# Choosing a head's sixteen experts on a grid of 112 sums and reading the two key numbers separately

## The chip, the cores and the metric

The kernel runs on one core of a Trainium2 chip. The metric is the device time of one execution in microseconds. Of the kernel before there are three timed runs, with a median of 3425.85 us (3422.84 to 3432.39). The engines are named as the profile names them: PE multiplies matrices (PEld is its weight load), DVE is the vector engine, ACT the scalar engine, POOL the GpSimd engine, and SP issues DMAs.

## What is computed

One block of a network over 1024 tokens and 16 prepended ones: an mLSTM and a forgetting attention side by side, an output projection, and then a retrieval of experts. The last part is the one that is changed. For each token and each of 8 heads, two halves of a query are scored against 128 keys each. The 16 best of each half are kept, all pairs of them are summed, and the 16 best sums name 16 experts out of 16384:

```python
val, idx = lax.top_k(scores, PEER_TOPK)
cand = (val[:, :, 0, :, None] + val[:, :, 1, None, :]).reshape(tb, PEER_HEADS, PEER_TOPK * PEER_TOPK)
cand_id = (idx[:, :, 0, :, None] * N_KEYS + idx[:, :, 1, None, :]).reshape(tb, PEER_HEADS, PEER_TOPK * PEER_TOPK)
top_s, pos = lax.top_k(cand, PEER_TOPK)
ids = jnp.take_along_axis(cand_id, pos, axis=-1).reshape(tb, PEER_HEADS * PEER_TOPK)
gate = jax.nn.softmax(top_s, axis=-1).reshape(tb, PEER_HEADS * PEER_TOPK)
...
act = jax.nn.gelu(jnp.einsum('ted,td->te', u, xb).astype(jnp.float32), approximate=False)
w = (gate * act).astype(xb.dtype)
return jnp.einsum('te,ted->td', w, v_emb[ids])
```

Since both lists of 16 are sorted from the best down, the pair (a, c) can be among the 16 best sums only if (a + 1)(c + 1) is at most 16. Fifty pairs fulfil that.

## The kernel before

The 1024 tokens are worked on in four segments of 256 (two blocks of 128 tokens, one token to a partition). A segment passes through its projections (proj), the mLSTM and the attention (mlstm, fox), the output projection and normalization (outp), and the choice of experts (topk). Then its experts are applied in one of two ways. Segments 0 and 3 fetch the rows of their experts from memory with indirect DMAs on POOL: a row of u for every choice (ask, L329, tile gu), which DVE multiplies with the token and sums (L338; for one block POOL multiplies 5 of 16, L335), and later four rows of v per group of tokens (L365, tile gv), which PE weighs and sums (L387, tile po). Segments 1 and 2 compute all 16384 experts densely in the last part of the program (dense_u, dense_v), with their choices spread out beforehand into a table G by the function gates: DVE, ACT and POOL make one-hot factors A and B (L1153, L1156, L1161), PE multiplies them (L1163, gout), ACT copies the result (L1165), and a DMA stores it (L1167, tile gd). One of the four B of each step is POOL's, the other three are DVE's. Besides, part of the dense first half is computed ahead into memory (spill, L999 to L1002, products at L293).

The function topk goes over the 8 heads: projections of the query (L886), scores (L891), and on DVE the 16 best of each half by two rounds of MAX, MAX_INDEX and MATCH_REPLACE over 128 scores (L898 to L903). Then it calls select once for each segment, so select runs 4 x 8 = 32 times, each time for two blocks. In select the 50 sums are laid out in rows of falling length by seven additions (L919 to L928, tile cand), and their expert numbers by seven more (tile cid, after L914 has multiplied the first half's numbers by 128). The 16 best of the 50 are taken by the same two rounds (L933 to L938), which give positions from 0 to 49 (pos). To read out the numbers at these positions, for each block and each 8 of the 16 positions a one-hot of 8 x 50 is made (L947), multiplied by cid (L949) and summed (L950); L951 turns the sums into integers in the table idx. Segment 0's choice runs beside segment 1's mLSTM and attention, that of segments 1 and 2 (one topk of both) beside segment 3's mLSTM and attention, and that of segment 3 beside the gates of segments 1 and 2 (L1194 to L1195).

What order the instructions have on each engine is not the order of the code: the program is recorded, and a planner with a simulated timeline then decides how the instructions of independent parts stand on each engine. On the chip each engine takes its instructions in that order. Segment 0's fetching of rows is recorded last (gather_first, L1196) and put by the planner into gaps; it may not start ahead of the end of segment 1's normalization (L1019). So a change of one function's instructions can move others.

Of the kernel before, what the change touches and what calls it, by code (L numbers as in the profile page):

```python
# [9 lines left out]
F32 = mybir.dt.float32  # L10
F32R = mybir.dt.float32r
I32 = mybir.dt.int32
U32 = mybir.dt.uint32
AF = mybir.ActivationFunctionType
OP = mybir.AluOpType
AX = mybir.AxisListType
# [3 lines left out]
P = 128  # L20
# [9 lines left out]
NH_P = 8  # L30
TOPK = 16
NE = 16384
NCAND = [(a, TOPK // (a + 1)) for a in range(TOPK)]
CAND = sum(n for _, n in NCAND)


def block_kernel(tc, I, out, dbg=None):
    nc = tc.nc
    with ExitStack() as ctx:
        _block_kernel(ctx, tc, nc, I, out, dbg)  # L40
# [44 lines left out]

RATE = 1.08
LAG = 5

OHB = 8
RAW = 4  # L90
WH = 2

# [1 line left out]
def _block_kernel(ctx, tc, nc, I, out, dbg):  # L94

    def pool(name, bufs, stack=ctx, **kw):
        return stack.enter_context(tc.tile_pool(name=name, bufs=bufs, **kw))
# [16 lines left out]
    tk = pool("topk", 2, mid)  # L114
# [24 lines left out]
    dve, act, pe, pool_e, sync = nc.vector, nc.scalar, nc.tensor, nc.gpsimd, nc.sync  # L139
# [33 lines left out]
    pool_e.iota(iota_i, pattern=[[1, P]], base=0, channel_multiplier=0)  # L173
    iota = cp.tile([P, P], F32, tag="iota", name="iota")
    dve.tensor_copy(iota, iota_i)
    iota_c = iota[:, 0:CAND]

    def tables(name):

# [84 lines left out]
    for i in range(3):  # L264
        c = slice(i * 512, min(L, i * 512 + 512))
# [644 lines left out]
    def select(h, S, val, ixu):  # L910
            nb, idx_i, gate = NB, S.idx, S.gate
            ixf = tk.tile([P, nb, 2, TOPK], F32, tag="ixf", name="ixf")
            dve.tensor_copy(ixf, ixu)
            dve.tensor_scalar(ixf[:, :, 0, :], ixf[:, :, 0, :], 128.0, None, op0=OP.mult)  # L914
            cand = tk.tile([P, nb, CAND], F32, tag="cand", name="cand")
            cid = tk.tile([P, nb, CAND], F32, tag="cid", name="cid", bufs=1)
            for dst, src in ((cand, val), (cid, ixf)):
                o = 0
                for a, nc_ in NCAND[:5]:  # L919
                    dve.tensor_tensor(dst[:, :, o:o + nc_], src[:, :, 0, a:a + 1].broadcast_to([P, nb, nc_]),  # L920
                                      src[:, :, 1, 0:nc_], op=OP.add)
                    o += nc_
                dve.tensor_tensor(dst[:, :, o:o + 6].rearrange("p b (a c) -> p b a c", a=3),
                                  src[:, :, 0, 5:8].unsqueeze(3).broadcast_to([P, nb, 3, 2]),
                                  src[:, :, 1, 0:2].unsqueeze(2).broadcast_to([P, nb, 3, 2]), op=OP.add)
                o += 6
                dve.tensor_tensor(dst[:, :, o:o + 8], src[:, :, 0, 8:16],
                                  src[:, :, 1, 0:1].broadcast_to([P, nb, 8]), op=OP.add)  # L928
            hs = slice(h * TOPK, (h + 1) * TOPK)
            top = gate[:, :, hs]  # L930
            pos = tk.tile([P, nb, TOPK], U32, tag="pos", name="pos", bufs=1)
            for b in range(nb):
                dve.max(top[:, b, 0:8], cand[:, b, :])  # L933
                dve.max_index(pos[:, b, 0:8], top[:, b, 0:8], cand[:, b, :])
                c2 = tk.tile([P, CAND], F32, tag="c2", name="c2")
                dve.match_replace(c2, top[:, b, 0:8], cand[:, b, :], -3.0e38)
                dve.max(top[:, b, 8:16], c2)
                dve.max_index(pos[:, b, 8:16], top[:, b, 8:16], c2)  # L938
            posf = tk.tile([P, nb, TOPK], F32, tag="posf", name="posf", bufs=1)
            dve.tensor_copy(posf, pos)  # L940
            idf = tk.tile([P, nb, TOPK], F32, tag="idfh", name="idfh", bufs=1)

            bc = [P, OHB, CAND]
            for b in range(nb):
                for r in range(0, TOPK, OHB):
                    oh = tk.tile(bc, F32, tag="oh", name="oh", bufs=1)
                    dve.tensor_tensor(oh, iota_c.unsqueeze(1).broadcast_to(bc),  # L947
                                      posf[:, b, r:r + OHB].unsqueeze(2).broadcast_to(bc), op=OP.is_equal)
                    dve.tensor_tensor(oh, oh, cid[:, b, :].unsqueeze(1).broadcast_to(bc), op=OP.mult)  # L949
                    dve.tensor_reduce(idf[:, b, r:r + OHB], oh, axis=AX.X, op=OP.add)  # L950
                dve.tensor_copy(idx_i[:, b, hs], idf[:, b, :])  # L951

    def softmax(S):
        nb, gate = NB, S.gate
# [26 lines left out]
    def main(S):  # L981
        yield from fox(S)
        yield from outp(S)
    def part(g, n):
        for _ in range(n):
            next(g)
            yield
# [76 lines left out]
    def chain(*gens):  # L1064
        for g in gens:
            yield from g
# [5 lines left out]
    for i in range(-1, len(SEGS)):  # L1072
# [3 lines left out]
        w = []  # L1076
# [5 lines left out]
        if i >= 0:  # L1082
# [10 lines left out]
            m, c = main(S), 8 + 3  # L1093
            if i == 0:
                T0 = topk(segs[0])
                m, c = chain(m, part(T0, T00)), c + T00
# [16 lines left out]
    nb, xb0, nx = 2 * NB, sum(SEGS[:DENSE[0]]), DX  # L1113
# [209 lines left out]
```

## Time and profile before

One execution was profiled. Its own time is 3424.24 us, and its span from the first to the last instruction 3422.4 us.

| | kernel before |
|---|---|
| median of 3 runs | 3425.85 us |
| profiled execution | 3424.24 us |
| its span | 3422.4 us |
| mean granted clock of PE | 0.926 |
| PE busy | 3040.1 us (89%) |
| DVE busy | 2294.6 us (67%) |
| POOL busy | 1523.4 us (45%) |
| ACT busy | 1066.8 us (31%) |
| DMA moved | 931.23 MB, mean 272 GB/s |

How to read it: the span has a front of about 2128 us, in which the four segments pass, segment 0's rows are fetched and the gates are made, and a dense part of about 1294 us, in which PE multiplies without a break worth naming. A share of busy time over the span says little, since the stages have different limits; the prediction goes stage by stage. In the views that are quoted, a row of a stage has the busy microseconds of each engine (with the number of its instructions as x), then the granted clock, the DMA engines' share, and GB/s. A row of a group has the line, engine, operation, output and inputs with their sizes, the number of instructions, their busy time and mean duration in ns, and then the idle time of the engine just ahead of them.

### The profile page before, as it was taken

How to read it: one execution, taken by the hardware profiler on the slowest of the kernel's cores; microseconds unless marked ns; L12 is line 12 of the kernel's file. 1: busy time of each engine (PE TensorE's matmuls, PEld its weight loads, DVE VectorE, ACT ScalarE, POOL GpSimd, SP SyncE). 2: the span in 40 equal slices, each digit the busy share in tenths (PEclk: the TensorE clock that was granted, in tenths of full speed). 3: DMA queues.
4: the chain of work that ended last, by engine and by line, in shares of the span. 5: the costliest groups of instructions: out<-in, count | busy, mean ns of one | idle time of the engine just before them, and what ended most of it. 6: DMA issues, size and time to landing. Idle time of an engine off the chain costs nothing. (4 is left out here: it accounts for less than half of the span.)

```text
span 3422.4 us, 42278 instructions
## 1 busy us (share of the span) xinstructions
PE 3040.1 (89%) x14225; PEld 2220.2 (65%) x14225; DVE 2294.6 (67%) x5970; ACT 1066.8 (31%) x2007; POOL 1523.4 (45%) x1321
## 2 busy tenths in 40 slices
PE   8899899878768868999998775999999999999999
PEld 4566677545535646676766553777777777777666
DVE  3242678577667999776788546788767677775443
ACT  1323424233333212222444553222322232322221
POOL 1000011177875777433565675454444545444442
PEclk9998899879679888999998886999999999999999
DMA  4444445579989999866787887888889999998995
GB/s 135 131 126 137 144 145 149 167 240 315 250 299 331 328 334 346 252 242 234 283 325 280 316 302 284 287 311 314 307 310 344 345 348 343 353 342 308 339 333 205
DMA packets 373821, 931.23 MB, mean 272 GB/s; under 512 B 57268, under 2 KB 143508, under 8 KB 371556
## 3 DMA queue, kind: packets, MB, share of 16 engines
q0 software_dynamic: 161216, 552.56, 45.9%
q1 hardware_dynamic: 212388, 375.96, 32.7%
q8 instruction: 113, 1.85, 0.2%
q14 instruction: 104, 0.85, 0.1%
HBM read 860.91 MB, written 67.47 MB: 271 GB/s over the span
## 5 line engine op out<-in xcount | busy, mean ns | idle before, releaser
L329 POOL DMA_INDIRECT gu<-in_peer_u,idx x512 | 626.3, 1223 | 521.1 <-PE vo L1258 110.0
L365 POOL DMA_INDIRECT gv<-in_peer_v,idT x512 | 546.0, 1066 | 593.1 <-PE po L387 314.3
L338 DVE SCALAR_TENSOR_TENSOR gu<-gu,xng 128x1024 f32<-128x1024 f32 x472 | 592.5, 1274 | 62.5 <-DMA gu<-in_peer_u,idx 60.6
L282 ACT CAST wh<-raw 128x1024 fp32r<-128x1024 f32 x288 | 302.1, 1049 | 884.2 <-PE vo L1258 270.9
L287 DVE TENSOR_TENSOR wl<-raw,wh 128x1024 fp32r<-128x1024 f32 x262 | 320.5, 1223 | 283.0 <-ACT wh L282 250.5
L1258 PE MATMUL vo<-wh,Wh 128*128 128x512 f32 x1024 | 376.7, 396 | 34.9 <-ACT Wh L1239 18.1
L1258 PE MATMUL vo<-wl,Wh 128*128 128x512 f32 x1024 | 402.6, 393 | 0.0
L1258 PE MATMUL vo<-wh,Wl 128*128 128x512 f32 x1024 | 400.3, 392 | 0.0
L387 PE MATMUL po<-gv,Z 128*32 128x512 f32 x2048 | 262.7, 606 | 19.1 <-DMA gv<-in_peer_v,idT 18.9
L306 PE MATMUL fp<-hnh,raw 128*128 128x256 f32 (+1 forms) x1024 | 251.4, 404 | 22.3 <-DVE frs L633 11.3
L1258 PEld LDWEIGHTS vo<-wh,Wh 128*128 128x128 f32 x1024 | 194.1, 190 | 98.3 <-issue 23.3
L293 PE MATMUL du<-xl,wh 128*128 128x512 f32 x640 | 250.3, 391 | 0.0
L293 PE MATMUL du<-xh,wl 128*128 128x512 f32 x640 | 250.2, 391 | 0.0
L293 PE MATMUL du<-xh,wh 128*128 128x512 f32 x640 | 249.8, 390 | 0.0
L306 PEld LDWEIGHTS fp<-hnh,raw 128*128 128x128 f32 x1024 | 203.8, 203 | 60.5 <-DVE frs L633 12.7
L1258 PEld LDWEIGHTS vo<-wl,Wh 128*128 128x128 f32 x1024 | 193.8, 189 | 48.6 <-issue 8.4
L1258 PEld LDWEIGHTS vo<-wh,Wl 128*128 128x128 f32 x1024 | 193.2, 189 | 48.1 <-issue 7.5
L1163 PE MATMUL gout<-A,B 128*128 128x128 f32 x1024 | 164.0, 319 | 67.6 <-POOL B L1161 62.9
L1163 PEld LDWEIGHTS gout<-A,B 128*128 128x128 f32 x1024 | 150.9, 226 | 103.6 <-POOL B L1161 76.6
L1165 ACT COPY G<-gout 128x512 f32<-128x512 f32 x128 | 136.4, 1066 | 202.0 <-PE gout L1163 195.4
L433 PE MATMUL tk<-raw,hnh 128*128 128x512 f32 (+1 forms) x416 | 197.4, 623 | 2.0 <-ACT vp L576 1.8
L1263 DVE TENSOR_TENSOR acc<-acc,vo 128x512 f32<-128x512 f32 x256 | 167.0, 683 | 32.8 <-PE vo L1258 29.1
(409 smaller groups left out, 5397.5 us busy)
## 6 DMA issues: line engine op xcount, KB each, us to landing
raw<-in_ut SPq DMA_DIRECT2D x128, 512.0 KB
raw<-in_peer_v SPq DMA_DIRECT2D x128, 512.0 KB
raw<-in_wf SPq DMA_DIRECT2D x64, 512.0 KB
gd<-G SPq DMA_DIRECT2D x16, 2048.0 KB
Gt<-gd SPq DMA_DIRECT2D x32, 1024.0 KB
raw<-in_wt SPq DMA_DIRECT2D x48, 512.0 KB
raw<-in_wq SPq DMA_DIRECT2D x48, 512.0 KB
raw<-in_wo SPq DMA_DIRECT2D x32, 512.0 KB
```

The source lines that it names most:

```text
L282: seen["act"] = act.copy(h, raw)
L287: seen["dve"] = dve.tensor_sub(l, raw, h.bitcast(F32))
L293: seen["pe"] = pe.matmul(o, w, x[:, c], start=(first and i == 0), stop=(last and i == 2))
L306: pe.matmul(o, raw[:, k * P:(k + 1) * P], xh[:, k, c], start=(k == 0), stop=(k == KT - 1))
L329: d = pool_e.indirect_dma_start(out=t, out_offset=None, in_=I["peer_u"], in_offset=bass.IndirectOffsetOnAxis(ap=S.idx[:, lb, r:r + 1], axi ...
L338: dve.scalar_tensor_tensor(t, t, 1.0, xn[0], op0=OP.mult, op1=OP.mult, accum_out=G.actv[:, r:r + 1])
L365: d = pool_e.indirect_dma_start(out=t, out_offset=None, in_=I["peer_v"], in_offset=bass.IndirectOffsetOnAxis(ap=S.idT[lb][:, tok:tok + 1], ...
L387: last = pe.matmul(G.po[32 * q_:32 * q_ + 32, n, :], z[:, q_, 31 - j:63 - j], rows[q_][:, n * 512:(n + 1) * 512], start=(j == 0), stop=(j ...
L433: pe.matmul(b[0:w, :], xh[:, k, s0:s0 + w], raw[:, k % 2 * 512:(k % 2 + 1) * 512], start=(k == 0), stop=(k == KT - 1))
L1163: pe.matmul(bk[:, u * P:(u + 1) * P], B[:, u, :], A[:, u, :], start=True, stop=True)
L1258: seen["pe"] = pe.matmul(bks[b], w[:, cw], v, start=(ii == 0 and i == 0), stop=(ii == GRP - 1 and i == 2))
L1263: dve.tensor_add(o, o, bks[b])
```

## The change

The candidates are laid out on a grid of 112 sums: all 16 partners for the best four of the first half, and the first four partners for the other twelve. The grid holds all fifty pairs. It is filled by two additions. A position p on it gives back its row and column by arithmetic: the row is the greater of p shifted right by 4 and (p shifted right by 2) - 12, and the column is p less the smaller of 16 x row and 4 x row + 48. The table cid of numbers goes away: row and column are each read out of the list of 16 numbers of their half, by a one-hot of 2 x 16 x 16 for each block, and a last instruction makes 128 x first + second as an integer. The second round of the choice works in place on cand.

```diff
-NCAND = [(a, TOPK // (a + 1)) for a in range(TOPK)]
-CAND = sum(n for _, n in NCAND)
+CAND = 4 * TOPK + 12 * 4
...
             dve.tensor_copy(ixf, ixu)
-            dve.tensor_scalar(ixf[:, :, 0, :], ixf[:, :, 0, :], 128.0, None, op0=OP.mult)
-            for dst, src in ((cand, val), (cid, ixf)):
-                o = 0
-                for a, nc_ in NCAND[:5]:
-                    dve.tensor_tensor(dst[:, :, o:o + nc_], src[:, :, 0, a:a + 1].broadcast_to([P, nb, nc_]),
-                                      src[:, :, 1, 0:nc_], op=OP.add)
...
+            for a0, a1, w in ((0, 4, TOPK), (4, TOPK, 4)):
+                bc = [P, nb, a1 - a0, w]
+                dve.tensor_tensor(cand[:, :, 48 * (a0 > 0) + a0 * 4:][:, :, 0:(a1 - a0) * w].rearrange("p b (a c) -> p b a c", c=w),
+                                  val[:, :, 0, a0:a1].unsqueeze(3).broadcast_to(bc),
+                                  val[:, :, 1, 0:w].unsqueeze(2).broadcast_to(bc), op=OP.add)
...
+            for k, n in ((1, 4), (2, 2)):
+                dve.tensor_scalar(pos[:, k], pos[:, 0], n, None, op0=OP.logical_shift_right)
+            pf = tk.tile([P, 3, nb, TOPK], F32, tag="posf", name="posf", bufs=1)
+            dve.tensor_copy(pf, pos)
+            dve.scalar_tensor_tensor(pf[:, 1], pf[:, 2], 12.0, pf[:, 1], op0=OP.subtract, op1=OP.max)
+
+            dve.tensor_scalar(pf[:, 2], pf[:, 1], 4.0, 48.0, op0=OP.mult, op1=OP.add)
+            dve.scalar_tensor_tensor(pf[:, 2], pf[:, 1], 16.0, pf[:, 2], op0=OP.mult, op1=OP.min)
+            dve.tensor_sub(pf[:, 2], pf[:, 0], pf[:, 2])
...
-            bc = [P, OHB, CAND]
             for b in range(nb):
-                for r in range(0, TOPK, OHB):
-                    oh = tk.tile(bc, F32, tag="oh", name="oh", bufs=1)
-                    dve.tensor_tensor(oh, iota_c.unsqueeze(1).broadcast_to(bc),
-                                      posf[:, b, r:r + OHB].unsqueeze(2).broadcast_to(bc), op=OP.is_equal)
-                    dve.tensor_tensor(oh, oh, cid[:, b, :].unsqueeze(1).broadcast_to(bc), op=OP.mult)
-                    dve.tensor_reduce(idf[:, b, r:r + OHB], oh, axis=AX.X, op=OP.add)
-                dve.tensor_copy(idx_i[:, b, hs], idf[:, b, :])
+                oh = tk.tile(bc, F32, tag="oh", name="oh", bufs=1)
+                dve.tensor_tensor(oh, iota[:, 0:TOPK].unsqueeze(1).unsqueeze(1).broadcast_to(bc),
+                                  pf[:, 1:3, b, :].unsqueeze(3).broadcast_to(bc), op=OP.is_equal)
+                dve.tensor_tensor(oh, oh, ixf[:, b].unsqueeze(2).broadcast_to(bc), op=OP.mult)
+                dve.tensor_reduce(idf[:, b], oh, axis=AX.X, op=OP.add)
+            dve.scalar_tensor_tensor(idx_i[:, :, hs], idf[:, :, 0, :], 128.0, idf[:, :, 1, :], op0=OP.mult, op1=OP.add)
```

The line numbers of the changed kernel are smaller: by 3 from the constants to select, and by 5 behind it.

**DVE, the first head of segment 0's choice.** These rows stand on DVE where the first select reads out its numbers, beside segment 1's mLSTM and the small projections of segment 2 (other lines). Before, from the conversion of the positions:

```order
L940 CAST posf<-pos 128x32
L692 SCALAR_TENSOR_TENSOR y<-nu__2316,sm,og 128x128 x3
L947 TENSOR_TENSOR oh<-iota,posf 128x400
L692 SCALAR_TENSOR_TENSOR y<-nu__2316,sm,og 128x128
L707 SCALAR_TENSOR_TENSOR Cst<-Cst,dec,mst 128x129
L949 TENSOR_TENSOR oh<-oh,cid 128x400
L508 SCALAR_TENSOR_TENSOR rb<-gx,ra 72x256
L950 TENSOR_REDUCE idfh<-oh 128x8
```

Now, at the same place:

```order
L929 TENSOR_SCALAR pos<-pos 128x32 x2
L497 SCALAR_TENSOR_TENSOR ra<-gx 72x256
L931 CAST posf<-pos 128x96
L704 SCALAR_TENSOR_TENSOR Cst<-Cst,dec,mst 128x129
L932 SCALAR_TENSOR_TENSOR posf<-posf 128x32
L934 TENSOR_SCALAR posf<-posf 128x32
L935 SCALAR_TENSOR_TENSOR posf<-posf 128x32
L936 TENSOR_TENSOR posf<-posf 128x32
L942 TENSOR_TENSOR oh<-iota,posf 128x512
L944 TENSOR_TENSOR oh<-oh,ixf 128x512
L505 SCALAR_TENSOR_TENSOR rb<-gx,ra 72x256
L945 TENSOR_REDUCE idfh<-oh 128x32
```

Six small instructions have come ahead of the read-out, and a round of the read-out has 512 elements where it had 400; there are two rounds in a select where there were four.

**POOL, during segment 3's attention.** kqa is the operand of an attention head, loaded by a DMA that POOL issues; gu and gv are segment 0's fetched rows, and wl is the lower half of a weight. Before, up to the load of the third head:

```order
L329 DMA gu<-in_peer_u,idx 128x1024 x13
L285 TENSOR_TENSOR wl<-raw,wh 128x1024
L329 DMA gu<-in_peer_u,idx 128x1024 x14
L285 TENSOR_TENSOR wl<-raw,wh 128x1024
L329 DMA gu<-in_peer_u,idx 128x1024 x5
L365 DMA gv<-in_peer_v,idT 128x1024 x4
L329 DMA gu<-in_peer_u,idx 128x1024 x10
L365 DMA gv<-in_peer_v,idT 128x1024 x4
L329 DMA gu<-in_peer_u,idx 128x1024
L285 TENSOR_TENSOR wl<-raw,wh 128x1024
L329 DMA gu<-in_peer_u,idx 128x1024 x3
L733 DMA kqa<-kd 66x2x1040
```

Now, up to the same load:

```order
L326 DMA gu<-in_peer_u,idx 128x1024 x14
L282 TENSOR_TENSOR wl<-raw,wh 128x1024
L326 DMA gu<-in_peer_u,idx 128x1024 x13
L282 TENSOR_TENSOR wl<-raw,wh 128x1024
L326 DMA gu<-in_peer_u,idx 128x1024 x4
L362 DMA gv<-in_peer_v,idT 128x1024 x4
L326 DMA gu<-in_peer_u,idx 128x1024 x8
L362 DMA gv<-in_peer_v,idT 128x1024 x4
L326 DMA gu<-in_peer_u,idx 128x1024 x2
L282 TENSOR_TENSOR wl<-raw,wh 128x1024
L326 DMA gu<-in_peer_u,idx 128x1024 x5
L730 DMA kqa<-kd 66x2x1040
```

Counted from the beginning of the program, 215 fetches of u stand ahead of this load before and 189 now; ahead of PE's first gout stand 224 po products (28 groups of four rows of v) before and now.

**POOL, at the end of the gates.** B is POOL's one of the four factors of a step. Before, up to the last B:

```order
L365 DMA gv<-in_peer_v,idT 128x1024 x4
L1161 TENSOR_SCALAR B<-iota,jT,gT 128x128
L329 DMA gu<-in_peer_u,idx 128x1024 x3
L1161 TENSOR_SCALAR B<-iota,jT,gT 128x128
L329 DMA gu<-in_peer_u,idx 128x1024 x3
L1161 TENSOR_SCALAR B<-iota,jT,gT 128x128 x4
L329 DMA gu<-in_peer_u,idx 128x1024 x6
L1161 TENSOR_SCALAR B<-iota,jT,gT 128x128
L329 DMA gu<-in_peer_u,idx 128x1024
```

Now, up to the last B and beyond it:

```order
L1156 TENSOR_SCALAR B<-iota,jT,gT 128x128
L326 DMA gu<-in_peer_u,idx 128x1024 x2
L1156 TENSOR_SCALAR B<-iota,jT,gT 128x128 x8
L362 DMA gv<-in_peer_v,idT 128x1024 x4
L1156 TENSOR_SCALAR B<-iota,jT,gT 128x128 x2
L326 DMA gu<-in_peer_u,idx 128x1024 x5
L1156 TENSOR_SCALAR B<-iota,jT,gT 128x128
L326 DMA gu<-in_peer_u,idx 128x1024 x121
```

The gu of these rows are segment 3's. Ahead of the last B stand 19 of them before and 7 now. On PE, 276 of the 512 gout products stand behind the last product of the spill before, and 256 now; 136 po products stand behind it in both. From the first dense product on, PE's order is the same in both. ACT loads its function tables 28 times before and 26 times now: the two loads that fall away stood between segment 2's Silu (L605) and an Exp of the attention (L781).

More of the change, by code (lines that the diff above doesn't have):

```diff
@@ L87 @@
 LAG = 5
-OHB = 8
 RAW = 4
@@ L175, in _block_kernel @@
     dve.tensor_copy(iota, iota_i)
-    iota_c = iota[:, 0:CAND]
     def tables(name):
@@ L913, in select @@
             dve.tensor_copy(ixf, ixu)
-            dve.tensor_scalar(ixf[:, :, 0, :], ixf[:, :, 0, :], 128.0, None, op0=OP.mult)
-            cand = tk.tile([P, nb, CAND], F32, tag="cand", name="cand")
-            cid = tk.tile([P, nb, CAND], F32, tag="cid", name="cid", bufs=1)
-            for dst, src in ((cand, val), (cid, ixf)):
-                o = 0
-                for a, nc_ in NCAND[:5]:
-                    dve.tensor_tensor(dst[:, :, o:o + nc_], src[:, :, 0, a:a + 1].broadcast_to([P, nb, nc_]),
-                                      src[:, :, 1, 0:nc_], op=OP.add)
[L922 to L928, printed above, removed]
+            cand = tk.tile([P, nb, CAND], F32, tag="cand", name="cand", bufs=1)
@@ L929, in select @@
+            for a0, a1, w in ((0, 4, TOPK), (4, TOPK, 4)):
[3 more added lines that the diff above has]
+                                  val[:, :, 1, 0:w].unsqueeze(2).broadcast_to(bc), op=OP.add)
             hs = slice(h * TOPK, (h + 1) * TOPK)
             top = gate[:, :, hs]
-            pos = tk.tile([P, nb, TOPK], U32, tag="pos", name="pos", bufs=1)
+            pos = tk.tile([P, 3, nb, TOPK], U32, tag="pos", name="pos", bufs=1)
@@ L932, in select @@
             for b in range(nb):
[L933 to L936, printed above, removed]
+                c2 = cand[:, b, :]
+                dve.max(top[:, b, 0:8], c2)
+                dve.max_index(pos[:, 0, b, 0:8], top[:, b, 0:8], c2)
+                dve.match_replace(c2, top[:, b, 0:8], c2, -3.0e38)
@@ L937, in select @@
                 dve.max(top[:, b, 8:16], c2)
[L938 to L941, printed above, removed]
-            bc = [P, OHB, CAND]
-            for b in range(nb):
-                for r in range(0, TOPK, OHB):
-                    oh = tk.tile(bc, F32, tag="oh", name="oh", bufs=1)
-                    dve.tensor_tensor(oh, iota_c.unsqueeze(1).broadcast_to(bc),
-                                      posf[:, b, r:r + OHB].unsqueeze(2).broadcast_to(bc), op=OP.is_equal)
-                    dve.tensor_tensor(oh, oh, cid[:, b, :].unsqueeze(1).broadcast_to(bc), op=OP.mult)
-                    dve.tensor_reduce(idf[:, b, r:r + OHB], oh, axis=AX.X, op=OP.add)
-                dve.tensor_copy(idx_i[:, b, hs], idf[:, b, :])
+                dve.max_index(pos[:, 0, b, 8:16], top[:, b, 8:16], c2)
@@ new lines, in select @@
+            dve.tensor_sub(pf[:, 2], pf[:, 0], pf[:, 2])
+            idf = tk.tile([P, nb, 2, TOPK], F32, tag="idfh", name="idfh", bufs=1)
+            bc = [P, 2, TOPK, TOPK]
+            for b in range(nb):
+                oh = tk.tile(bc, F32, tag="oh", name="oh", bufs=1)
[3 more added lines that the diff above has]
+                dve.tensor_reduce(idf[:, b], oh, axis=AX.X, op=OP.add)
```

## The prediction

> **What bounds the kernel now.** I read the page first (PE 89% busy, DVE 67%), and then cut the span into stages, because such shares mean little over work with different limits. The cuts follow where the selects and the gates lie. Columns: busy us of PE, PEld, DVE, ACT, POOL, granted clock of PE, DMA share, GB/s.
>
> ```profile
> 0.00:350.00 350.00, 321.73 (x1174) 206.37 (x1175) 119.53 (x371) 101.50 (x268) 25.02 (x57) 0.93 0.47 135
> 350.00:650.00 300.00, 267.83 (x1341) 209.12 (x1340) 222.51 (x900) 104.53 (x248) 22.93 (x21) 0.91 0.47 139
> 650.00:1075.00 425.00, 307.21 (x1130) 206.30 (x1129) 273.81 (x507) 139.61 (x328) 300.54 (x216) 0.80 0.87 278
> 1075.00:1375.00 300.00, 240.76 (x1117) 185.99 (x1116) 296.14 (x945) 70.65 (x140) 214.18 (x162) 0.86 0.97 337
> 1375.00:1650.00 275.00, 259.43 (x1277) 180.64 (x1276) 186.52 (x752) 70.20 (x124) 98.16 (x87) 0.97 0.74 248
> 1650.00:1910.00 260.00, 240.18 (x1408) 179.02 (x1407) 224.52 (x920) 115.88 (x228) 150.92 (x146) 0.95 0.79 293
> 1910.00:2128.00 218.00, 132.24 (x796) 94.52 (x795) 114.79 (x316) 105.39 (x213) 149.03 (x141) 0.78 0.82 302
> 2128.00:3422.00 1294.00, 1270.67 (x5994) 958.20 (x5994) 856.75 (x1264) 359.05 (x461) 562.65 (x493) 0.99 0.89 319
> ```
>
> The last 1294 us are PE's (1271 busy) and keep their order, so nothing is to be had there. Of the rest, PE is the limit up to 350, and nearly so from 1375 to 1910. From 1075 to 1375 DVE is busy 296 of 300 us, PE only 241. From 1910 to 2128 neither is full. The same stages with the second product of the read-out alone (L949, four to a select) tell where the selects are:
>
> ```profile
> 350.00:650.00 300.00, 18.23 (x32) 0.91 0.47 139
> ...
> 1075.00:1375.00 300.00, 18.50 (x30) 0.86 0.97 337
> 1375.00:1650.00 275.00, 22.27 (x34) 0.97 0.74 248
> 1650.00:1910.00 260.00, 18.38 (x32) 0.95 0.79 293
> ```
>
> So 8, 7.5, 8.5 and 8 of the 32 selects. In DVE's own stage, these are PE's waits:
>
> ```profile
> PE fm L747 <- DVE mx L753: 15.1, 7, 5.3
> PE sc L891 <- ACT qT L888: 9.2, 3, 6.8
> PE fmT L758 <- DVE Zm L755: 7.6, 2, 4.9
> PE mst L706 <- DVE Cst L707: 7.3, 3, 5.1
> ...
> PE fmT L758 <- DVE mx L753: 3.4, 2, 2.5
> ```
>
> Those on DVE add up to 15.1 + 7.6 + 7.3 + 3.4 = 33 us of the 59 us that PE stands idle: attention and mLSTM wait for small DVE results that are queued behind row sums and selects.
>
> **What one select costs DVE, before and after.** The groups by shape, and DVE in order of time in one select:
>
> ```profile
> L949 DVE TENSOR_TENSOR oh<-oh,cid 128x400 f32<-128x400 f32 x128 | 77.4, 605 | 1.9
> L950 DVE TENSOR_REDUCE idfh<-oh 128x8 f32<-128x400 f32 x128 | 71.8, 561 | 1.6
> L899 DVE FIND_INDEX8 ixu<-val,sc 128x8 uint32<-128x128 f32 x128 | 35.1, 283 | 0.0
> L934 DVE FIND_INDEX8 pos<-gate,cand 128x8 uint32<-128x50 f32 x64 | 13.1, 204 | 0.0
> L676 DVE TENSOR_TENSOR nu__4858<-nu__4858,m 128x129 f32<-128x129 f32 x4 | 1.2, 288 | 2.6 <-issue 1.9 <-ACT nu__4858 L675 0.7
> L914 DVE TENSOR_SCALAR ixf<-ixf 128x32 f32<-128x32 f32 x32 | 5.7, 179 | 0.0
> ```
>
> ```profile
> 510.63 0.50 DVE L920 TENSOR_TENSOR cid<-ixf 128x32 f32<-128x32 f32 x5
> 511.05 0.16 DVE L923 TENSOR_TENSOR cid<-ixf 128x12 f32<-128x12 f32 x1
> ...
> 513.68 0.57 DVE L949 TENSOR_TENSOR oh<-oh,cid 128x400 f32<-128x400 f32 x1
> 514.29 0.57 DVE L950 TENSOR_REDUCE idfh<-oh 128x8 f32<-128x400 f32 x1
> 514.89 0.57 DVE L947 TENSOR_TENSOR oh<-iota,posf 128x400 f32<-128x400 f32 x1
> ```
>
> - An element costs (283 - 204) / (128 - 50) = 1.01 ns.
> - Read-out: dependent steps start 0.605 us apart (513.68, 514.29, 514.89). Before 12 of them, 7.26 us. Now 6 with 112 elements more, 0.605 + 0.113 = 0.72 us each, 4.31 us. Saved 2.95.
> - Small additions: five start within 511.05 - 510.63 = 0.42 us, so 0.084 each, independent ones overlapping in part. Fourteen of them and L914 are 15 x 0.084 = 1.26 us. The two new ones have 2 x 4 x 16 = 128 and 2 x 12 x 4 = 96 elements; by the 128x129 row (288 ns, less about 0.07 of overlap) 0.40 us for both. Saved 0.86.
> - The choice of 16: ten passes over 62 elements more, 10 x 62 x 1.01 ns. Added 0.63. They take the same loads of match values as before.
> - Undoing the position: six more small instructions and 64 more elements in the conversion. Overlapped they would cost 6 x 0.084 = 0.5 us, as a strict chain 6 x 0.18 (L914) = 1.08. It is nearly a chain, so 0.9 + 0.06; nothing but DVE's other work can stand between.
> - The end: two conversions become one instruction of the same kind. Saved 0.1.
>
> Sum 2.95 + 0.86 - 0.63 - 0.96 + 0.1 = 2.3 us of DVE for a select, 74 us over 32. Ends: 1.7 (two-input products at 0.76, the strict chain), and 3.4 if each removed addition had held DVE for its whole duration of 0.16.
>
> The Trainium skill, "VectorE: DVE Perf Modes", section "The DRAIN you can't avoid", has the next instruction wait until the pipe is empty and advises a smaller count of instructions; the same page lets one that is not held start earlier. By the first rule alone the sum would be the upper end, 3.4 us a select. The row of five additions in 0.50 us speaks for the second.
>
> **What of it reaches the end.**
>
> Segment 0's choice (350 to 650): 8 x 2.3 = 18 us less of 222 on DVE. PE is idle 32 us there, and its waits on DVE are:
>
> ```profile
> PE fp L306 <- DVE frs L633: 8.2, 2, 5.8
> ...
> PE fmT L758 <- DVE mx L753: 3.1, 2, 2.8
> ```
>
> That is 11.3 us; I take 4, between nothing and 11, nearer to DVE's share of the load that goes. Two table loads on ACT go as well; ACT is busy 105 of the 300 us and hides them.
>
> DVE's stage (1075 to 1375): 7.5 x 2.3 = 17 us less. DVE is full, so its chain gets shorter by that; PE gets back the part of its idle time that hangs on DVE, 33 of 59. I take 0.6 x 17 = 10, between 0 (if the fetches hold) and 17.
>
> From 1375 to 1650 PE is the limit (259 of 275): the 20 us of DVE that go there were cover already. 0.
>
> Gates, first part (1650 to 1910): PE has 240 of 260. The planner puts five more steps of the gates ahead of the last spill product (256 gout products behind it in place of 276). Twenty products cost PE 20 x 2 x 0.16 = 6 us there (two records to a product, and 164.0 us for 1024 records):
>
> ```profile
> L1163 PE MATMUL gout<-A,B 128*128 128x128 f32 x1024 | 164.0, 319 | 67.6 <-POOL B L1161 62.9
> ```
>
> Loss 6, gain by lighter DVE up to 6; I take -4.
>
> Gates, second part (1910 to 2112): POOL's groups in this stretch, busy and then idle time ahead of them, fill it:
>
> ```profile
> L1161 POOL TENSOR_SCALAR B<-iota,jT,gT 128x128 f32<-128x128 f32 x65 | 69.2, 1067 | 21.0 <-PE gout L1163 19.2 <-DMA gv<-in_peer_v,idT 0.5 <-POOL B L1161 0.2
> L365 POOL DMA_INDIRECT gv<-in_peer_v,idT x57 | 57.4, 1008 | 26.5 <-PE po L387 14.2 <-issue 9.7 <-PE gout L1163 2.3
> L329 POOL DMA_INDIRECT gu<-in_peer_u,idx x19 | 23.0, 1213 | 4.7 <-issue 3.4 <-DVE B L1161 0.5 <-DVE A L1153 0.5
> ```
>
> 69.2 + 21.0 + 57.4 + 26.5 + 23.0 + 4.7 = 202 us: POOL's queue is the stage. A B takes 90.2 / 65 = 1.39 us with its wait, a gu 27.7 / 19 = 1.46. The changed order has 5 B and 12 gu fewer ahead of its last B: 5 x 1.39 + 12 x 1.46 = 24.5. The gu go behind the last B, where POOL now stands idle. I take 20, between 0 and 24.
>
> Sum: 4 + 10 + 0 - 4 + 20 = 30 us. The profiled execution took 3424.24 us (span 3422.4 and 1.8 around it), 1.6 below the median of 3425.85. Forecast 3424 - 30 = **3394 us**; with the ends of the terms set against each other, 3375 to 3408.
>
> **Rivals.**
>
> *The fetches hold.* From 1075 to 1375 the DMA share is 0.97 at 337 GB/s; a lighter DVE would only wait for rows. Against it: from 1910 to 2128 a share of 0.82 moved 302 GB/s, so a full share may move 368, 9% more. Then that term is 0, POOL's order gives half of its 20, and the first part of the gates still loses 4: 4 + 0 - 4 + 10 = 10 us, 3414 us. Chance 0.20.
>
> *The clock comes along.* PE's granted clock is 0.86 in DVE's stage, where PE idles, and 0.99 in the tail, where it doesn't. With the waits on DVE gone, 241 us of products at 0.86 would take 241 x 0.86 / 0.95 = 218 (0.95 as from 1650 to 1910). With 17 us in place of 10 and half of those 23 us: 30 + 7 + 12 = 49, 3375 us. Chance 0.12. The Trainium skill, "TensorE: Matmul & The Clock Gate", section "Part 1: The HAM clock gate (the "warmup" mystery)", says that the clock halves after an idle window of about 3.4 us and comes back with activity; the waits of 4.9 to 5.3 us above are of the length that it means.
>
> *PE comes too early (slower).* Between 1075 and 1910 PE's products for segment 0 (po) stand at fixed places in its order, 28 groups ahead of the first gout, and the third attention head of segment 3 now stands behind 189 fetches of u, not 215. PE moves up against fetches that can't, and then holds everything behind a po. It decides from 30 / 28 = 1.1 us of added wait per group; at 1.6 us it costs 45, and the time is 3394 + 45 = 3439 us. Against it: DMA has a share of only 0.74 from 1375 to 1650. Chance 0.10.
>
> *DVE isn't lighter.* If the chain for the positions and the longer choice eat the gain (0.6 us and below for a select), only the new order is left, which may fall either way: 3424, within 8 us. Chance 0.08.
>
> **How the numbers follow.** Forecast 0.50, the rivals 0.20, 0.12, 0.10 and 0.08. A measurement can tell about 0.3%, 10 us, from no change. Faster by more: 0.50 + 0.12 and six tenths of 0.20, 0.74. Within: the other 0.08 and most of the last rival, 0.14. Slower: 0.12. The range reaches from 3362 (the clock's case with its upper ends) to 3426, which leaves out the slower case, half of the last one, and a little below: under 0.2.
>
> **What would show it.** Right: in the changed profile a select has six read-out steps of about 0.72 us; DVE's total falls by 60 to 110 us; the stretch in which DVE is full ends 10 us or more earlier; from the last spill product to the last gout it takes about 180 us, not 202; the dense part keeps its 1294 us. Wrong: PE's waits for fetched rows at L387 grow past 1 us a group; DVE's full stretch is as long as before with waits on gu; or POOL waits longer for po to free its rows in the second part of the gates.

## The result, and the profile after

The changed kernel takes **3373.68 us** (median of 4 runs, 3370.77 to 3378.99), the kernel before 3428.85 us over 4 runs taken with them. The ratio is 0.9843 with a 95% interval of 0.9822 to 0.9863: 55 us faster by the medians, where 30 were forecast. The profiled execution of the changed kernel took 3372.53 us, 51.7 less than that of before. In its page DVE's total is 63 us lower than before (2294.6), POOL's is much the same, and so is PE's:

```profile
PE 3030.4 (90%) x14225; PEld 2215.6 (66%) x14225; DVE 2231.5 (66%) x5522; ACT 1063.7 (32%) x2005; POOL 1518.4 (45%) x1321
```

The stages of the changed kernel, cut at about the same places of the program as before (busy us of PE, PEld, DVE, ACT, POOL, then granted clock, DMA share, GB/s):

```profile
349.00:645.00 296.00, 261.36 (x1335) 204.44 (x1335) 208.06 (x788) 101.96 (x245) 22.88 (x21) 0.93 0.49 141
645.00:1045.00 400.00, 301.39 (x1093) 205.71 (x1092) 269.40 (x480) 139.28 (x328) 286.31 (x204) 0.78 0.87 283
1045.00:1345.00 300.00, 262.62 (x1269) 201.13 (x1267) 272.76 (x834) 77.03 (x154) 200.28 (x163) 0.88 0.97 326
1345.00:1620.00 275.00, 245.21 (x1156) 171.04 (x1157) 183.49 (x664) 64.76 (x109) 119.24 (x101) 0.93 0.80 276
1620.00:1870.00 250.00, 245.10 (x1482) 180.47 (x1481) 215.49 (x837) 128.03 (x253) 164.88 (x155) 1.00 0.88 323
1870.00:2073.00 203.00, 118.95 (x723) 85.77 (x723) 104.94 (x286) 91.68 (x188) 135.33 (x129) 0.78 0.82 307
2073.00:3370.00 1297.00, 1275.11 (x5994) 961.17 (x5994) 857.70 (x1264) 358.82 (x461) 564.41 (x493) 0.99 0.89 318
```

DVE is no longer full in the third of these (273 of 300 us), but the DMA engines are, at 0.97 as before. In that stretch PE's waits on DVE have shrunk; the largest of them, fm for mx, was 15.1 us before and is 4.8 now (total us, times, longest):

```profile
PE fmT L755 <- DVE Zm L752: 6.9, 3, 3.9
PE fm L744 <- DVE mx L750: 4.8, 6, 2.1
PE m L693 <- DVE y L689: 3.0, 1, 3.0
```

A select costs what was worked out for it. In the groups by shape and in DVE's order of time (start, duration) the read-out has six steps, 0.72 to 0.73 us apart (the first three are shown):

```profile
L942 DVE TENSOR_TENSOR oh<-iota,posf 128x512 f32<-128x512 f32 x64 | 48.0, 750 | 1.0
L944 DVE TENSOR_TENSOR oh<-oh,ixf 128x512 f32<-128x512 f32 x64 | 46.5, 726 | 1.0
```

```profile
510.12 0.19 DVE L935 SCALAR_TENSOR_TENSOR posf<-posf 128x32 f32<-128x32 f32 x1
...
510.35 0.18 DVE L936 TENSOR_TENSOR posf<-posf 128x32 f32<-128x32 f32 x1
...
510.57 0.69 DVE L942 TENSOR_TENSOR oh<-iota,posf 128x512 f32<-128x512 f32 x1
511.30 0.69 DVE L944 TENSOR_TENSOR oh<-oh,ixf 128x512 f32<-128x512 f32 x1
512.02 0.69 DVE L945 TENSOR_REDUCE idfh<-oh 128x32 f32<-128x512 f32 x1
```

If each DVE instruction of a select is counted until it ends or the next one starts, a select held DVE for 10.50 us before and holds it for 8.17 now: 2.33 us less, 75 us over 32. DVE's total fell by less, 63 us, since the other instructions together held it 12 us longer.

Where did the time go? The program has marks that both kernels pass: the last transposed piece of each segment's normalization (L858 before, L855 after), the last spill product, the last and the first product of the two following stages (gout, vo). The stages between them, in us of the profiled executions:

| stage | before | after | forecast |
|---|---|---|---|
| A: to segment 0 normalized | 370.2 | 370.2 | 0 |
| B: to segment 1 normalized (segment 0's choice) | 300.0 | 295.0 | -4 |
| C: to segment 2 normalized (no select in it) | 383.3 | 359.7 | 0 |
| D: to segment 3 normalized (choices of 1 and 2) | 582.5 | 583.1 | -10 |
| E: to the last spill product (gates, segment 3's choice) | 270.9 | 259.6 | +4 |
| F: to the last gout | 203.0 | 170.7 | -20 |
| G: to the first vo | 18.5 | 34.8 | 0 |
| H: dense part | 1294.0 | 1297.6 | 0 |

The sum is near, but the parts are not. D, DVE's stage, gained nothing; C, in which no select runs, gained 24 us; F gained 32; and G lost 16. Only the cost of a select came out as it was worked out. B is near, too, but its 5 us are no more than a stage differs by from one execution to the next, as the runs below show.

### The profile page after: what moved, and what is told of

Its sections match the earlier page's. It is cut to its first block, busy times and chain, and to the rows that moved or that the text cites. A ratio compares the mean times of both kernels' runs of the same rounds, so it can differ in the third digit from the quotient of the medians.

```text
span 3370.8 us, 41849 instructions
## 1 busy us (share of the span) xinstructions
PE 3030.4 (90%) x14225; PEld 2215.6 (66%) x14225; DVE 2231.5 (66%) x5522; ACT 1063.7 (32%) x2005; POOL 1518.4 (45%) x1321
## 5 line engine op out<-in xcount | busy, mean ns | idle before, releaser
L326 POOL DMA_INDIRECT gu<-in_peer_u,idx x512 | 611.9, 1195 | 529.0 <-DVE gu L335 107.6
L362 POOL DMA_INDIRECT gv<-in_peer_v,idT x512 | 556.4, 1087 | 536.4 <-PE po L384 296.2
L335 DVE SCALAR_TENSOR_TENSOR gu<-gu,xng 128x1024 f32<-128x1024 f32 x472 | 610.0, 1310 | 59.9 <-DMA gu<-in_peer_u,idx 59.0
L1258 DVE TENSOR_TENSOR acc<-acc,vo 128x512 f32<-128x512 f32 x256 | 167.6, 684 | 34.6 <-PE vo L1253 34.3
```

What stands on the lines that cost most here:

```text
L326: d = pool_e.indirect_dma_start(out=t, out_offset=None, in_=I["peer_u"], in_offset=bass.IndirectOffsetOnAxis(ap=S.idx[:, lb, r:r + 1], axi ...
L335: dve.scalar_tensor_tensor(t, t, 1.0, xn[0], op0=OP.mult, op1=OP.mult, accum_out=G.actv[:, r:r + 1])
L362: d = pool_e.indirect_dma_start(out=t, out_offset=None, in_=I["peer_v"], in_offset=bass.IndirectOffsetOnAxis(ap=S.idT[lb][:, tok:tok + 1], ...
L1258: dve.tensor_add(o, o, bks[b])
```

## The experiments

Each of the first four changes the planner's order of all engines; in the later ones the order is held, or changes only near the dense part. First: is it DVE's load at all, or the order? Theory A below is that a lighter DVE makes the gain, except for the part that hangs on where the gates stand. Rival B is that the planner's new order makes it, whatever DVE does.

### Load put back, and two small disturbances, each in an order of its own

The changed kernel with three more passes of its own in a select:

```diff
-                dve.tensor_tensor(oh, iota[:, 0:TOPK].unsqueeze(1).unsqueeze(1).broadcast_to(bc),
-                                  pf[:, 1:3, b, :].unsqueeze(3).broadcast_to(bc), op=OP.is_equal)
+                for _ in range(2 + b):
+                    dve.tensor_tensor(oh, iota[:, 0:TOPK].unsqueeze(1).unsqueeze(1).broadcast_to(bc),
+                                      pf[:, 1:3, b, :].unsqueeze(3).broadcast_to(bc), op=OP.is_equal)
```

> The changed kernel with three more of its own read-out comparisons in a select (128x512, 750 ns each in the profile of the changed kernel, at most 2.2 us of DVE in all), so that a select costs DVE about what it did before (10.5 us of DVE's own time, against 8.2 in the changed one). Their results are overwritten. Theory A (a lighter DVE makes the gain): it goes back to 3420 to 3430 us less the part that hangs on where the gates stand, so 3405 to 3430, and the last transposed pieces of segment 2 come back from 1025 towards 1055 us. Rival B (the planner's new order makes most of it, whatever DVE does): it stays at 3365 to 3385, or moves by as much as a kernel does that has one more small copy in a select.

The changed kernel, and then the kernel before, with one small copy more in a select:

```diff
             dve.tensor_copy(pf, pos)
+            dve.tensor_copy(pf[:, 0], pos[:, 0])
```

> The changed kernel with one more small copy in a select (the first third of the positions, converted twice; about 0.1 us of DVE, 3 us over 32 selects). The planner gives it another order of all engines. Theory A: 3374 us plus 0 to 4. Rival B: anywhere, by 20 us or more to either side, and the part from the last transposed pieces of segment 1 to those of segment 2 (361 us in the changed kernel, 386 before) changes as much as it did with the change.

```diff
             dve.tensor_copy(posf, pos)
+            dve.tensor_copy(posf, pos)
```

> The kernel before with one more small copy in a select (the positions converted twice; about 0.1 us of DVE). The planner gives it another order. Theory A: 3429 us plus 0 to 4. Rival B: off by 20 us or more to either side.

The old select in the changed kernel, in the tiles of the new one (CAND is 112 there and CAND0 is 50; the positions and comparisons lie in the new tiles in the same way):

```diff
+            both = tk.tile([P, nb, CAND], F32, tag="cand", name="cand", bufs=1).rearrange("p b c -> p (b c)")
+            cand = both[:, 0:nb * CAND0].rearrange("p (b c) -> p b c", b=nb)
+            cid = both[:, nb * CAND0:2 * nb * CAND0].rearrange("p (b c) -> p b c", b=nb)
...
```

> The old select, instruction for instruction, in the changed kernel, its candidates, positions and comparisons laid into the tiles of the new one (one buffer of candidates in place of two). It shows whether the smaller or single buffers do anything, and gives one more order of the same work. Theory A: 3429 us within 10. Rival B: off by 20 us or more. If the tiles mattered, near 3374.

Measured, against 3429.57 us for the kernel before (13 runs beside them):

| kernel | us | ratio, 95% interval |
|---|---|---|
| changed, three passes more | 3397.95 | 0.9906 (0.9887 to 0.9924) |
| changed, one copy more | 3428.02 | 0.9996 (0.9985 to 1.0007) |
| before, one copy more | 3400.54 | 0.9924 (0.9908 to 0.9941) |
| before, in the new tiles | 3393.86 | 0.9907 (0.9884 to 0.9929) |

A copy that adds 5 us of DVE in all took away the changed kernel's whole gain; the same kind of copy made the kernel before 29 us faster. A changed kernel with three passes more (74 us of DVE, its page says 2305.3) is faster than one with a copy; its 3398 lies between the forecasts of A and B. On the whole rival B had it right: **another order from the planner moves the time by 30 to 50 us, either way**, and a single comparison of two kernels cannot tell a lighter DVE from a luckier order. In one point B missed: it expected the copy to move C as much as the change did, and C took 364 us, 5 more than in the changed kernel. Theory A as stated had fallen.

### The order held: new select in the old order, old select in the new

So the order was taken out of the planner's hands. The order of one kernel was written down and every engine's instructions were chained in it, without waits:

```diff
+        for one, two in zip(row, row[1:]):
+            assert one.engine == two.engine
+            tc.add_manual_dep(two, one.name, mybir.DependencyInfo(
+                mybir.DependencyClass.NoSync, mybir.DependencyReason.DATA), reason="order")
```

PE, ACT, POOL, SP and DVE's other instructions stand exactly as in the kernel whose order it is. A select of another length is spread over the old places. That changes what it costs: with the new select in the order of before DVE's total is 2251.3 us, so 43 less than before, not 63; with the old one in the changed order it is 2323.5, so 92 more than in the changed kernel.

> The changed select with every engine held to the order of the kernel before: PE, ACT, POOL and SyncE instruction for instruction, DVE's other instructions as well, and the new select's 27 instructions spread over the places at which the old one's 41 stood (their number lists have three buffers in place of two, for this order). Only DVE's load differs from before. Theory A (lighter DVE): 15 to 30 us faster than before, 3400 to 3415. Theory B (the planner's order made the 55 us): 3429 within 8.

> The mirror image: the old select with every engine held to the order of the changed kernel, its 41 instructions laid over the places of the new one's 27 (number lists with three buffers). Only DVE's load differs from the changed kernel. Theory A: 15 to 30 us slower than the changed kernel, 3389 to 3404, or more, since an order made for short selects lets long ones hold up what stands behind them. Theory B: 3374 within 8.

| | order of before | order of the changed kernel |
|---|---|---|
| old select | 3428.6 | 3428.0, ratio 0.9999 (0.9985 to 1.0012) |
| new select | 3417.1, ratio 0.9975 (0.9964 to 0.9986) | 3373.7, ratio 0.9843 (0.9822 to 0.9863) |

Neither theory gave all of this. A DVE that is 43 us lighter is worth 11.5 us in the old order by the medians, 9 by the ratio (5 to 12); the changed order with the old select is worth nothing; both together 55. The stage rows say why. C, D, and E with F, first of before, then of the new select in the order of before:

```profile
670.00:1053.00 383.00, 270.42 (x987) 181.82 (x986) 253.83 (x460) 125.08 (x295) 284.34 (x202) 0.79 0.88 283
1053.00:1636.00 583.00, 509.71 (x2429) 373.93 (x2429) 489.09 (x1710) 143.59 (x265) 322.89 (x258) 0.91 0.87 293
1636.00:2110.00 474.00, 384.20 (x2264) 281.92 (x2262) 339.41 (x1241) 224.22 (x451) 304.25 (x289) 0.89 0.80 299
```

```profile
671.00:1056.00 385.00, 279.05 (x985) 188.15 (x985) 252.34 (x459) 125.03 (x294) 284.95 (x202) 0.76 0.87 281
1056.00:1639.00 583.00, 508.40 (x2429) 373.97 (x2428) 467.01 (x1486) 143.24 (x265) 317.11 (x258) 0.91 0.87 293
1639.00:2104.00 465.00, 382.18 (x2262) 281.45 (x2261) 328.49 (x1129) 224.44 (x451) 301.30 (x289) 0.89 0.81 305
```

In D, DVE is 22 us lighter (489 to 467) and the stage takes the same 583. What is gained in the profiled execution lies in the gates (9 us) and perhaps in B (3); A, C and H, in which no select runs, took 8 of it back, 2 to 4 us each. And then the changed order, first with its own select, and then with the old one in it:

```profile
665.00:1025.00 360.00, 266.79 (x976) 183.02 (x974) 252.78 (x450) 125.34 (x294) 276.48 (x194) 0.78 0.88 289
1025.00:1608.00 583.00, 515.36 (x2443) 377.55 (x2442) 459.09 (x1496) 143.81 (x265) 323.85 (x267) 0.90 0.89 301
1608.00:2038.00 430.00, 371.72 (x2244) 273.57 (x2243) 307.28 (x1106) 222.68 (x451) 291.97 (x277) 0.93 0.84 313
```

```profile
685.00:1041.00 356.00, 262.58 (x972) 180.06 (x971) 253.39 (x449) 125.09 (x294) 275.30 (x193) 0.78 0.89 290
1041.00:1655.00 614.00, 522.14 (x2445) 382.57 (x2444) 504.24 (x1720) 143.87 (x265) 322.62 (x267) 0.88 0.85 286
1655.00:2099.00 444.00, 377.57 (x2244) 273.69 (x2243) 331.81 (x1218) 223.45 (x451) 290.07 (x278) 0.92 0.82 302
```

C takes 356 to 360 us in the changed order and 383 to 386 in the old one, whichever select the kernel has. With the old select the changed order then loses 12 us in B and 31 in D against the kernel before.

### The same order with a copy, and with three passes

The old select's 41 instructions were crowded onto 27 places, so the loss could be the crowding. The copy and the three passes of the first runs need none of that: each stands right behind the instruction that it repeats.

> The changed kernel with the same one more small copy in a select that took 3428 us in an order of its own, now with every engine held to the order of the changed kernel, the copy right behind the conversion that it repeats. If the order alone made those 54 us: 3374 to 3380. If the copy itself costs them: 3428.

> The changed kernel with the three further read-out comparisons in a select that took 3398 us in an order of its own, now with every engine held to the order of the changed kernel, each comparison right behind the one that it repeats. DVE alone is loaded as before, at the same places. If it was DVE's load that cost the old select 54 us in this order: 3405 to 3428. If it was the laying of 41 instructions over 27 places: 3374 to 3390.

The copy: 3384.26 us, ratio 0.9890 (0.9844 to 0.9937), against 3428.02 in the order of its own; DVE's total is the same in both (2236.5 and 2236.6). So of the 54 us between the changed kernel and that one, 36 by the ratios and 44 by the medians are the order's. The three passes: 3411.79 us, ratio 0.9961 (0.9941 to 0.9980). With DVE loaded as before, the changed order loses 38 of its 55 us. It was DVE's load, then; the crowding, with which DVE's total is 19 us higher still (2323.5 against 2304.1), can account for no more than the remaining 16. The copy's time was expected at 3374 to 3380 if the order alone counted; the 11 us by which its median exceeds the changed kernel's are not clear of noise, since the intervals overlap.

### The same test in a third order

The order of the kernel before with its copy (3400.5 us) was held, first with the very instructions of the kernel before, then with the new select.

> The kernel before, not one instruction more or less, held to the order that the planner wrote for it with one more small copy in a select (that kernel took 3400.5 us); the copy itself is left out. If the order alone is worth the 28 us: 3398 to 3401, with no DVE work saved at all. If not: 3429.

> The new select held to that same other order (as in the run of the new select in the order of before: its 27 instructions over the places of the old 41, number lists with three buffers). With the run just ahead it gives what the lighter DVE is worth at one more fixed order. If it is worth about what it was in the order of before: 11 us less, 3387 to 3392. If an order for long selects gives nothing to short ones: 3398 to 3402. Theory A as first stated: 3370 to 3385.

Before, reordered: **3389.71 us**, ratio 0.9882 (0.9858 to 0.9906), 38 us faster than the kernel before beside it (3427.78) with not one instruction less, and 8 less than the least that was expected. The new select in the same order: 3396.22, ratio 0.9897 (0.9873 to 0.9922). The intervals overlap, so a lighter DVE shows no gain here. It is 31 us lighter, not 75, since the new select again costs more at the old one's places. The first rows of the two pages:

```profile
PE 3041.1 (90%) x14225; PEld 2221.1 (66%) x14225; DVE 2290.8 (68%) x5970; ACT 1067.1 (32%) x2007; POOL 1521.4 (45%) x1321
```

```profile
PE 3038.0 (89%) x14225; PEld 2220.9 (65%) x14225; DVE 2260.1 (67%) x5522; ACT 1067.2 (31%) x2007; POOL 1516.0 (45%) x1321
```

The stages of all held runs, side by side, with DVE's total:

| select, order | DVE | A | B | C | D | E | F | G |
|---|---|---|---|---|---|---|---|---|
| old, of before | 2294.6 | 370.2 | 300.0 | 383.3 | 582.5 | 270.9 | 203.0 | 18.5 |
| new, of before | 2251.3 | 373.7 | 297.0 | 385.6 | 582.8 | 261.9 | 203.2 | 18.3 |
| new, of changed | 2231.5 | 370.2 | 295.0 | 359.7 | 583.1 | 259.6 | 170.7 | 34.8 |
| new and copy, of changed | 2236.5 | 373.6 | 300.4 | 355.6 | 590.9 | 261.1 | 169.2 | 34.3 |
| new and 3 passes, of changed | 2304.1 | 373.7 | 307.1 | 361.3 | 597.2 | 268.8 | 170.4 | 34.6 |
| old, of changed | 2323.5 | 372.8 | 312.2 | 356.3 | 613.9 | 274.8 | 169.3 | 35.2 |
| old, third order | 2290.8 | 371.6 | 300.3 | 356.7 | 587.1 | 260.3 | 193.1 | 22.1 |
| new, third order | 2260.1 | 375.3 | 300.4 | 358.0 | 585.5 | 266.6 | 191.9 | 22.1 |

Each row is one execution, and A, in which no select runs, differs by 5 us between them; so differences of that size say nothing. The two runs of the next section, in which the changed kernel's order is the same up to the end of E, agree: they have 300.1 and 295.3 for B, 586.1 and 584.7 for D.

This table is the answer. **C, F and G follow the order alone**: within one order they agree to a few microseconds, whatever the select costs. **B, D and E follow DVE's load in the changed order**. In the old order only E does, by 9 us, and in the third none gains; E is even 6 us longer there with the new select.

What the old order has in C that the changed one lacks shows in DVE's waits there. Sums over fetched rows (gu), 92 of them in the old order and 88 in the changed one, and wv stand in DVE's queue ahead of segment 2's normalization, and in the old order they wait longer: gu for its rows, wv for ACT. First before, then the new select in its order, then the changed kernel (total us, times, longest):

```profile
DVE gu L338 <- DMA gu<-in_peer_u,idx: 39.4, 16, 7.9
...
DVE wv L346 <- ACT wv L343: 9.7, 1, 9.7
```

```profile
DVE gu L335 <- DMA gu<-in_peer_u,idx: 40.1, 18, 6.4
...
DVE wv L343 <- ACT wv L340: 9.7, 1, 9.7
```

```profile
DVE gu L335 <- DMA gu<-in_peer_u,idx: 25.6, 14, 5.2
...
DVE wv L343 <- ACT wv L340: 1.7, 1, 1.7
```

49 and 50 us of such waits with the two selects in the old order, 27 in the changed one. In the third order, where C is as short, 88 sums stand ahead and the same two rows make 26 and 24 us. That goes with the 24 us of C; that it is all of the cause was not tried apart.

### The gap ahead of the dense part

G lost 16 us with the changed order. The chain of the kernel before has the last store of gates and the first load of them:

```profile
2111.43 7.29 DMA gd<-G
2118.80 8.16 DMA Gt<-gd
```

and that of the changed kernel:

```profile
2041.79 7.41 DMA gu<-in_peer_u,idx
2049.38 22.39 DMA Gt<-gd
```

The first Gt (1 MB) needs 22.4 us in place of 8.2. The fetches of u that had stood between the B's now stand behind the last one, beside that load, and four loads of acc (2 MB) are ahead of it in SP's queue, as before. Two edits, the second on top of the first:

```diff
-    for b in range(nb):
-        sync.dma_start(acc[:, b, :], h2d[xs0 + b * P:xs0 + (b + 1) * P, :])
...
         W = weights(g)
+        if g == 0:
+            for b in range(nb):
+                sync.dma_start(acc[:, b, :], h2d[xs0 + b * P:xs0 + (b + 1) * P, :])
```

> The changed kernel, with the four loads of the dense part's starting sums (acc, 4 x 512 KB) behind the first load of gates (Gt) in SyncE's queue, not ahead of it; nothing else of the order differs up to there. In the changed kernel the first Gt takes 22.4 us to land behind them and beside 16 fetches of u. If the bytes ahead of it are what it waits for: 2 MB at the 0.42 MB a us of that stretch, 5 us less, 3369. If the fetches alone hold it: 3374 within 2.

```diff
         ws.append(dense_u(i))
-        beat(2)
...
-        sync.dma_start(Gt, gd[:, :, e0:e0 + GRP, :].rearrange("b j i t -> j b i t"))
+        ld = sync.dma_start(Gt, gd[:, :, e0:e0 + GRP, :].rearrange("b j i t -> j b i t"))
+        if g == 0:
+            seen["pe"], pe_ = ld, seen["pe"]
+            for _ in range(AHEAD):
+                beat(2)
+            seen["pe"] = pe_
```

> As the run before, and the fetches of u that stood between the last B and the dense part wait until the first Gt has landed. If those fetches are what held Gt: it lands in 8 us as before, 14 to 19 us less in all, 3355 to 3360. The rival: the rows come later, the pace of the dense part is held by them, and the gain is lost before the end: 3374 within 4 or slower.

With acc behind Gt: 3365.82 us, ratio 0.9832 (0.9812 to 0.9853). The load takes 18.0 us and G 29.5, the 5 us expected. The whole time is 8 us less by the medians, but its interval overlaps the changed kernel's, so only the stage shows it:

```profile
2052.70 17.98 DMA Gt<-gd
```

With the fetches held as well: **3348.36 us**, ratio 0.9777 (0.9761 to 0.9793), 25 us less than the changed kernel, where 14 to 19 were expected, and the fastest of all. The first multiplication that needs Gt starts 6.25 us after SP issued it at 2039.25, and the first fetch follows it:

```profile
2039.25 0.37 SPq L1224 DMA_DIRECT2D Gt<-gd  x1
```

```profile
2045.50 2.50 DVE L1233 TENSOR_TENSOR w<-w,Gt 128x512 f32<-128x512 f32 x4 [7.29 <-DMA Gt<-gd]
2045.73 1.34 POOL L326 DMA_INDIRECT gu<-in_peer_u,idx  x1 [17.83 <-DMA Gt<-gd]
```

G is 17.6 us, and F has become 9.6 us shorter too, since the last fetches no longer stand ahead of the last B on POOL. The dense part took 1296.2 us: the later rows were not missed.

## Why the prediction was right in its time and wrong in much of its reasoning

The measured 3374 lies in the range of 3362 to 3426, 20 us under the forecast of 3394. That it came so near is in good part luck: D's 10 us did not come and G cost 16 that were not foreseen, while C gave 24, F 12 and E 15 more than worked out. Point by point:

- **A select's cost.** 2.3 us less were worked out (1.7 to 3.4), 2.33 came. The steps of 0.72 us, the overlap of the small additions and the near chain for the positions hold. The chain itself starts its steps 0.22 us apart (510.12, 510.35, 510.57), where 0.18 were taken. Counted term by term as above, the read-out saved 2.5 us (2.95 worked out), the additions 1.1 (0.86) and the end 0.4 (0.1); the choice added 0.6 and the positions 1.0, as worked out. So errors that cancel helped the sum. By the rule cited from the Trainium skill, "VectorE: DVE Perf Modes", section "The DRAIN you can't avoid", the sum would have been 3.4; the 2.33 speak for overlapping small instructions, as the row of five additions did.
- **B, "I take 4".** 5.0 in the changed kernel, 3.0 at the old order. That agrees, but it isn't shown: the same order with the same select gave 300.1 in the run with acc behind Gt, as much as before.
- **DVE's stage, "I take 0.6 x 17 = 10".** The step that failed: D took 583.1 us in place of 582.5. "PE gets back the part of its idle time that hangs on DVE" looked no farther than the stretch in which DVE was full. There PE did get more done in the changed kernel (262.6 us busy for 240.8), but less in the 275 us behind that (245.2 for 259.4), and the stage ended no earlier. With the new select in the old order D takes 582.8 us with 22 us less of DVE, but that run does not tell what holds the stretch, since little of the 22 came off in it. The stretch that was 1075 to 1375 is

```profile
1078.00:1378.00 300.00, 241.00 (x1121) 187.52 (x1124) 291.92 (x839) 70.08 (x139) 206.77 (x162) 0.86 0.97 338
```

  with DVE at 292 us where it had 296, and PE at 241 us, a clock of 0.86 and a DMA share of 0.97, all three as before. PE's largest wait on DVE there, 15.1 us before, is as long:

```profile
PE fm L744 <- DVE mx L750: 16.8, 4, 5.8
```

  In the changed order D does follow DVE's load (583, 591, 597 and 614 us). Of the rivals, *the fetches hold* had this term at 0; that the fetches are what holds it wasn't tried by itself.
- **C, nothing.** No term at all was given to a stage without a select. Its 24 us are the order's, as the held runs show. This is the largest thing that was missed: moves were looked for at two or three places, though the planner had rewritten every engine's order.
- **Gates, first part, +4.** 11 us faster instead. At the old order a lighter DVE gives 9 of them, where "gain by lighter DVE up to 6" was allowed; in the third order it gives none.
- **Gates, second part, -20.** The mechanism was right and stands apart from DVE: 203.0 and 203.2 us with either select in the old order, 169 to 171 in the changed one. The size is 32. The working counted 5 B and 12 gu; in POOL's groups from 1870 to 2041

```profile
L1156 POOL TENSOR_SCALAR B<-iota,jT,gT 128x128 f32<-128x128 f32 x60 | 62.7, 1048 | 21.1 <-PE gout L1158 18.2 <-POOL B L1156 1.8
L362 POOL DMA_INDIRECT gv<-in_peer_v,idT x50 | 51.3, 1027 | 21.8 <-PE po L384 10.7 <-issue 5.7 <-PE gout L1158 4.8
L326 POOL DMA_INDIRECT gu<-in_peer_u,idx x8 | 8.9, 1116 | 2.0 <-PE gout L1158 1.1 <-issue 0.9
```

  there are also 50 gv where there were 57. At the old row's (57.4 + 26.5) / 57 = 1.47 us each, 7 of them are an estimated 10 us more: 24.5 and 10 against the 32 measured. Counted behind the last spill product, as the stages are here, 268 gout and 136 po products stood there before and 240 and 120 do now.
- **"The gu go behind the last B, where POOL now stands idle."** POOL did, the DMA engines didn't: a cost of 16 us in G was put at nothing, for want of asking what else is to be loaded there.
- **The clock comes along** gave 3375, the measured time, by another mechanism. The clock of the whole span is 0.927 after 0.926, and that of D 0.90 after 0.91. Whether waits of 5 us lower it was not tried in any run. **PE comes too early** (slower): PE's waits for rows of v between D's end and the last gout fell from 12.7 us to 1.5:

```profile
PE po L387 <- DMA gv<-in_peer_v,idT: 12.7, 4, 5.1
```

```profile
PE po L384 <- DMA gv<-in_peer_v,idT: 1.5, 1, 1.5
```

So of the 52 us between the profiled executions, C, F and G make 40, and the held runs give them to the order. B, D and E make 16 (H gives back 4), and a DVE that is 43 us lighter, at the old order, makes 12 in B, D and E, of which 9 in E are clear of the scatter. In the changed order the 40 can't be had without the lighter DVE: put the load back, and that order loses most or all of them in B, D and E. The third order shows that this need not be so: it gives 38 us to the old select. What stays open is whether short selects make good orders likelier. In orders of the planner's own the old select took 3429, 3401 and 3394 us, the new one 3374 and 3428 (3398 with three passes more); that is too few to tell.

## What to carry to other kernels

Where a planner with a simulated timeline orders the program, any edit draws a new order, and here a copy of 5 us in all was worth 30 to 50 us of it: time a change together with a null edit or two, or hold the order, before its gain is put down to what it does. Time that is regained in the stretch in which an engine is full isn't yet time off the program: follow it to the end of the stage. To see what load alone is worth, hold the order, and then read from the profile how much load really went: here instructions laid over another kernel's places saved 43 and 31 us of DVE, not 63. And where work is moved behind a point, ask what is loaded from memory there, not only which engine stands idle.

## What was not expected of the hardware

A load of 1 MB by SP's queue landed in 8.2 us in the kernel before, and in 22.4 us with fetches on POOL's queue beside it and the same 2 MB ahead of it; without the 2 MB it took 18.0, and with neither its first user started 6.25 us after the issue. What DVE's load costs depends on the order: in the changed one 73 us more cost 38 us (5 us more cost 11 by the medians, not clear of noise), while in the third order 31 us less brought nothing. The same new select, instruction for instruction, gave DVE totals of 2231.5, 2251.3 and 2260.1 us in three orders.
